# Reordering the first projections of a hybrid attention kernel: the second token pair, the last value weights, and two remainders

## The chip, the cores and the metric

One core of a Trainium2 chip runs the whole program. The metric is the device time of one execution in microseconds (us); the kernel before takes 1420.7 us, the median of three runs between 1420.46 and 1420.71.

The core has five engines with a queue each: TensorE (PE in the profile, its weight loads PEld), VectorE (DVE), ScalarE (ACT), GpSimd (POOL) and SyncE (SP, which issues most of the loads). An engine works through its queue in order; an instruction that needs the result of another engine waits in its place.

## The reference

The layer normalises the input, projects it with one wide matrix, runs two branches on it, merges them by gates, and ends in an MLP and a last normalisation. Only the beginning matters for this change:

```
def hybrid_layer(x, layer, norm1_g, w_in, ...):
    xn = rmsnorm(x, norm1_g[layer])
    u = xn @ w_in[layer].astype(f32)
    c = np.cumsum([SB_WIDTH, SB_WIDTH, SB_WIDTH, HG_WIDTH, HG_WIDTH, HG_WIDTH, HG_WIDTH, D_MODEL])
    q_sb, k_sb, v_sb, f_raw, i_hg, q_hg, g_hg, gate_sb, gate_hg = jnp.split(u, list(c), axis=-1)
    o_sb = stick_breaking_attention(split_heads(q_sb, SB_HEADS), split_heads(k_sb, SB_HEADS),
                                    split_heads(v_sb, SB_HEADS))
    ...
    merged = g_a * (o_sb @ w_o_sb[layer].astype(f32)) + g_b * (o_hg @ w_o_hg[layer].astype(f32))
    h = x.astype(f32) + merged @ w_out[layer].astype(f32)
    ...
    a = jnp.square(jax.nn.relu(hn @ w_ff1[layer].astype(f32)))
    h = h + a @ w_ff2[layer].astype(f32)
    return h
```

There are 1024 tokens of width 1024. `rmsnorm` divides a token by the root of its mean square and multiplies each column by a gain. The first head's queries and keys (64 columns each) and all values (512 columns) are what the first part of the program computes.

## The kernel before

**Two-part numbers.** A float32 operand is split into a high part, rounded to TensorE's `fp32r` format, and a low part, the remainder. A product is three matmuls: high by high, low by high, high by low. The high part is a cast on ScalarE (`hi_copy`, L156), the remainder a subtraction on VectorE (`lo_sub`, L161) that reads the raw tile and the high part.

**The input.** Tokens come in eight blocks of 128 (`x0` to `x7`; block 2 and block 3 are called x_165 and x_169 in the built program). A block's mean square is taken half on ScalarE and half on VectorE (`half_means`), GpSimd raises it to the power -1/2 (`inv_root`, L274), VectorE multiplies the block by that (`norm1`, L664). TensorE transposes it in eight column groups kt of 128 columns (`norm_transpose`, L131), one PSUM bank `xnt` to a group; from there ScalarE writes the high part with the gain applied (`xnh`, L348) and VectorE the low part (`xnl`, L351). A tile of xnh and of xnl holds two groups: 229/230 the groups 0 and 1, 237/238 the groups 2 and 3, 245/246 the groups 4 and 5, 253/254 the groups 6 and 7. Blocks 0 and 1 are the first pair, 2 and 3 the second, 4 to 7 the second half.

**The first job.** `first_job` makes a generator that advances one step at a time. It computes the first head's query/key product `pjqk` (weights `wqk0whi`, `wqk0wlo`) and the values `pjv`, one PSUM bank to a token block. The value weights come in four pieces of two column groups each: raw `wvr`, high `wvh`, remainder `wvl`; piece 0 serves groups 0 and 1, piece 3 the groups 6 and 7. In the kernel before, its steps are: the first pair's query/key (four steps), pieces 0 and 1 of the values of blocks 0 and 1 with the high weights (two steps), the same with the remainders (two steps), the second pair's query/key (four steps), then the values' other pieces and the remaining blocks.

**What sets the order.** The main program calls `st.advance(n, 1)` for n steps between its own parts, and this fixes each queue up to that point. `lo_now` issues subtractions that were put off in `owed_wlo`; before, that is piece 1's `wvl` alone. `turns` chains the instructions of ScalarE and of VectorE in the order in which they are written; `after` records such an order for the compiler and adds no wait on the chip. The loads on SyncE are in the order x0, x1, norm gains, wqk0, wvr 0, x2, wvr 1, x3, wvr 2, wvr 3, x4 to x7.

The main program around the change, before:

```
    st.advance(4, 1)
    u_v.split(2)
    norm1((2, 3), half_means((2, 3)))
    lo_now()
    st.advance(3, 1)
    norm_transpose(xn, 0, 2, 2)
    u_v.split()
    st.advance(5, 1)
```

Of the kernel before, what the change touches and what calls it, by code (L numbers as in the profile page):

```python
# [9 lines left out]
F32 = mybir.dt.float32  # L10
# [4 lines left out]
ALU = mybir.AluOpType  # L15
# [24 lines left out]
def kernel(  # L40
# [19 lines left out]
    nc = tc.nc  # L60
# [14 lines left out]
    def slot(name, dt=F32):  # L75
        return spool.tile([P, 1024], dt, tag="s", name=name)
# [7 lines left out]
    def bank(name):  # L84
        return psum.tile([P, 512], F32, tag="p", name=name)
# [19 lines left out]
    def after(ins, earlier):  # L105
        if earlier is not None and earlier.ins is not ins.ins:
            tc.add_manual_dep(ins.ins, earlier.ins.name, NOSYNC, reason="issue order")
        return ins

    def open_block(name):  # L110
        cur[0] = name
        lane = lanes[name]
        lane.gates = (lane.last,)
        if name == "main":
            lane.ends.append(lane.last)
        else:
            ends = lanes["main"].ends
            lane.gates += tuple(ends[-AHEAD : len(ends) - AHEAD + 1])
# [11 lines left out]
    def transpose(dst, src):  # L130
        return pe(nc.tensor.transpose(dst, src, ident))  # L131
# [7 lines left out]
    last_lo, attended, owed_wlo = [None], [None], []  # L139

    def lo_now(behind=None):
        while owed_wlo:
            after(owed_wlo.pop()(), behind)

    turns = {"on": False, "act": None, "dve": None}

    def in_turn(engine, ins):
        if turns["on"]:
            after(ins, turns[engine])
            turns[engine] = ins  # L150
        return ins
# [3 lines left out]
    def hi_copy(dst, src):  # L155
        hi_last[0] = after(in_turn("act", nc.scalar.copy(dst, src)), hi_behind[0])  # L156

    def lo_sub(dst, src, hi):
        return in_turn(
            "dve",  # L160
            nc.vector.tensor_tensor(out=dst, in0=src, in1=hi.bitcast(F32), op=ALU.subtract),  # L161
        )

    def hi_lo(h, l, src):
        hi_copy(h, src)
        return lo_sub(l, src, h)
# [16 lines left out]
    def halves():  # L183
        return ((i, slice(i * 512, (i + 1) * 512)) for i in range(2))
# [134 lines left out]
            c = (kt % 2) * 512 + (tb % 4) * P  # L319
            return h[:, c : c + P], l[:, c : c + P]  # L320

    def norm_transpose(acts, half, b0, n, between=None):

        banks = {}

        def turn_block(kt, b):
            if kt not in banks:
                banks[kt] = bank(f"xnt{half}{kt}_{b0}")[:, 0 : n * P]
            open_block("main")
            transpose(  # L330
                banks[kt][:, b * P : (b + 1) * P],
                xt[4 * half + b0 + b][:, kt * P : (kt + 1) * P],
            )

        ahead = 6 if between else 0
        for kt in range(ahead):
            turn_block(kt, 0)
        if between:
            between()
        for kt in range(KT):  # L340
            hi, lo = acts.t.get((half, kt // 2)) or acts.make(half, kt // 2)
            cs = slice(kt % 2 * 512 + b0 * P, kt % 2 * 512 + (b0 + n) * P)
            for b in range(n):
                if b > 0 or kt >= ahead:
                    turn_block(kt, b)
            pb = banks[kt]
            g = prm[:, G1 + kt : G1 + kt + 1]
            in_turn("act", nc.scalar.activation(hi[:, cs], pb, AF.Identity, scale=g))  # L348
            in_turn(
                "dve",  # L350
                nc.vector.scalar_tensor_tensor(  # L351
                    out=lo[:, cs],
                    in0=pb,
                    scalar=g,
                    in1=hi[:, cs].bitcast(F32),
                    op0=ALU.mult,
                    op1=ALU.subtract,
                ),
            )

    class Quads:

# [82 lines left out]
    class Unit:  # L445
# [28 lines left out]
        def split(self, upto=None):  # L474
            self.load(upto)
            self.hl = self.hl or []
            for i, r in list(enumerate(self.raw))[len(self.hl) : upto]:
                if self.wide:
                    h = slot(f"{self.name}h{i}", F32R)
                    l = slot(f"{self.name}l{i}", F32R)  # L480
                else:
                    h = wpool.tile([P, 1024], F32R, tag="whi", name=f"{self.name}h{i}")
                    l = wpool.tile([P, 1024], F32R, tag="wlo", name=f"{self.name}l{i}")
                self.hl.append((h, l))
                if self.name == "wf1" or self.name == "wv" and i == 1:
                    hi_copy(h, r)
                    owed_wlo.append(lambda h=h, l=l, r=r: lo_sub(l, r, h))
                    continue
                after(after(hi_lo(h, l, r), last_lo[0]), attended[0])

# [73 lines left out]
    st = Stream()  # L564
# [54 lines left out]
    xn = Acts("xn")  # L619

    def half_means(tbs):
        (l, lc), (r, rc) = halves()
        means = {}
        for tb in tbs:
            t, scr = xt[tb], slot(f"n1scr{tb}")
            ssq = small.tile([P, 1], F32, tag="ssq1", name=f"n1_{tb}_ss", bufs=4)
            in_turn(
                "act",
                nc.scalar.activation(
                    scr[:, lc], t[:, lc], AF.Square, scale=D ** -0.5, accum_out=ssq  # L630
                ),
            )
            ms = mean_square(scr[:, rc], t[:, rc], EPS, f"n1_{tb}")
            in_turn("dve", add(ms, ms, ssq))
            means[tb] = inv_root(ms, f"n1_{tb}")
        return means
# [21 lines left out]
    def norm1(tbs, means=None):  # L658
        for tb in tbs:
            t = xt[tb]  # L660
            r = means[tb] if means else token_rstd(t, f"n1_{tb}", slot(f"n1scr{tb}"))
            in_turn(
                "dve",
                nc.vector.tensor_scalar(out=t, in0=t, scalar1=r, scalar2=None, op0=ALU.mult),  # L664
            )
# [58 lines left out]
    def first_job():  # L724
        name, u_qk, ep = qk_item(0)
        u_qk.__class__ = FirstUnit
        u_v = wide_unit("wv", W_IN, C_V, 512)
        u_v.roomy = range(4)
        open_banks = {}

        def v_part(tb, kt, hi=True, lo=True):
            if kt == 0 and hi:
                open_banks[tb] = bank(f"pjv_{tb}")
            ps = open_banks[tb]
            sh, sl = xn.stat(kt, tb)
            wh, wl = (w[:, kt % 2 * 512 : (kt % 2 + 1) * 512] for w in u_v.hl[kt // 2])
            if hi:
                matmul(ps, sh, wh, start=kt == 0, stop=False)
                matmul(ps, sl, wh, start=False, stop=False)
            if lo:  # L740
                matmul(ps, sh, wl, start=False, stop=kt == KT - 1)

        def v_steps(tb, kts):
            for kt in kts:
                v_part(tb, kt)
                if kt == KT - 1:
                    v_epilogue(open_banks.pop(tb), tb)
                if kt % 2 == 1:
                    yield

        def qk_steps(ps, half, b0, n):
            ts = slice(b0 * P, (b0 + n) * P)
            return proj_half(ps[:, ts], u_qk.hl[0], xn.mov, KT, half, ts=ts)

        def body():
            ps = bank(f"{name}_0")
            yield from qk_steps(ps, 0, 0, 2)
            for hi in (True, False):
                for k0 in (0, 2):
                    for tb in range(2):  # L760
                        for kt in (k0, k0 + 1):
                            v_part(tb, kt, hi, not hi)
                    yield
            yield from qk_steps(ps, 0, 2, 2)
            ep(ps, 0)
            st.prefetch()
            for tb in range(4):
                yield from v_steps(tb, range(4, KT) if tb < 2 else range(KT))
            ps = bank(f"{name}_1")
            yield from qk_steps(ps, 1, 0, 4)  # L770
            ep(ps, 1)
            for tb in range(4, NT):
                yield from v_steps(tb, range(KT))

        return st.add([u_qk], body), u_qk, u_v

    j_first, u_qk0, u_v = first_job()
    j_qk = {0: j_first}

# [1549 lines left out]
    st.advance(4, 1)  # L2329
    u_v.split(2)  # L2330
    norm1((2, 3), half_means((2, 3)))
    lo_now()
    st.advance(3, 1)
    norm_transpose(xn, 0, 2, 2)
    u_v.split()
    st.advance(5, 1)
    norm1(range(4, NT))
    st.advance(8, 1)
    norm_transpose(xn, 1, 0, 4)
# [16 lines left out]
    for i, it in enumerate(items):  # L2356
# [12 lines left out]
        def between():  # L2369
            if before:  # L2370
                values(*before)

        r = turn(*it, between)
# [135 lines left out]
```

## Time and profile before

| | before |
|---|---|
| median of three runs | 1420.7 us |
| the profiled execution | 1420.47 us |
| its span, first to last instruction | 1418.7 us |
| TensorE busy | 1408.6 us, 99% |
| VectorE busy | 1088.1 us, 77% |
| ScalarE busy | 684.6 us, 48% |
| GpSimd busy | 143.3 us, 10% |
| granted TensorE clock | 0.999 of full speed |

The profile is of one execution. Its views list the instructions by engine and group, in the order of time, or by what an engine waited for. In a row of the order of time stand the start, the duration, the engine, the line, the operation, output and inputs by name, shapes and count; in brackets how long the engine had idled before and what ended that. A row with a count above one joins like instructions that follow each other. Matmuls overlap, and their ends are modelled, so the distance between two starts says more than a duration. A row of the waits names the engine and its instruction, what it waited for, the microseconds in total, how often, and the longest. A row of the groups has the busy time and the mean in ns behind the first bar. A row of the stretches has the bounds, the length, the busy time of each engine with its number of instructions, the granted clock, the share of the DMA engines and the GB/s.

### The profile page before, as it was taken

Reading aid. Unit: us, or ns where it says so; the run is one execution under the profiler, and the core shown is the slowest. Engines: PE = TensorE matmul, PEld = TensorE weight load, DVE = VectorE, ACT = ScalarE, POOL = GpSimd, SP = SyncE. Lnnn points to the kernel's source line nnn. Section 1 sums busy time; section 2 is a strip of 40 time slices with the busy share of each in tenths; the row PEclk is TensorE's granted clock in tenths of the full one; section 3 lists DMA queues with packets and bytes.
Section 4 is the critical chain, followed back from the end, with each engine's and each line's share of the span. In section 5 each row is a group of like instructions: output and inputs, shape, how many; then the busy total and the mean of one; then the engine's idle time right before and its main releaser. Section 6 shows DMA issues by size and latency. Waiting matters only on the chain.

```text
span 1418.7 us, 18796 instructions
## 1 busy us (share of the span) xinstructions
PE 1408.6 (99%) x6848; PEld 1184.0 (83%) x6848; DVE 1088.1 (77%) x1494; ACT 684.6 (48%) x1182; POOL 143.3 (10%) x339
## 2 busy tenths in 40 slices
PE   9999999999999999999999999999999999999998
PEld 8888888888888888888888888888888888888886
DVE  7579988988567888887788897677766657768766
ACT  6356676664243554433334764445444443434343
POOL 3012223210011031000000300000000000000031
PEclk9999999999999999999999999999999999999999
DMA  7124445545135685364585514444446974776725
GB/s 238 30 67 127 105 100 98 106 76 155 62 74 167 227 222 182 124 215 156 160 299 193 185 53 170 163 162 139 143 144 239 351 268 152 278 273 240 277 93 187
DMA packets 163173, 237.72 MB, mean 168 GB/s; under 512 B 26332, under 2 KB 93448, under 8 KB 163080
## 3 DMA queue, kind: packets, MB, share of 16 engines
q1 hardware_dynamic: 146056, 190.37, 40.0%
q0 software_dynamic: 11584, 34.61, 10.0%
q10 hardware_dynamic: 5440, 11.54, 2.3%
q8 instruction: 54, 0.88, 0.3%
q14 instruction: 39, 0.32, 0.1%
HBM read 168.32 MB, written 66.06 MB: 165 GB/s over the span
## 4 chain that ended last, share of the span: by engine, by line
PE 98%; DVE 1%; ACT 1%; DMA 0%; issue 0%; POOL 0%; SPq 0%; POOLq 0%; DVEq 0%; ACTq 0%
PE pm L128 21%; PE pX L128 9%; PE pW L128 6%; PE pY L128 6%; PE pjqk L128 6%; PE pga L128 4%; PE gX L128 4%; PE gY L128 4%; PE pjf L128 3%; PE pjq L128 3%; PE pys L128 3%; PE pji L128 3%; PE pyh L128 3%; PE pjv L128 3%; PE po L128 3%; PE z L128 2%
## 5 line engine op out<-in xcount | busy, mean ns | idle before, releaser
L156 ACT CAST whid<-w 128x1024 fp32r<-128x1024 f32 x30 | 31.6, 1054 | 154.4 <-PE pm L128 89.7
L826 DVE TENSOR_TENSOR_SCAN rm<-rm,bits 128x511 f32<-128x511 f32 (+7 forms) x72 | 87.3, 1220 | 17.0 <-ACT rm L804 16.9
L128 PE MATMUL pm<-whid,sh 128*128 128x512 f32 x240 | 93.4, 389 | 0.0
L128 PE MATMUL pm<-wlod,sh 128*128 128x512 f32 x240 | 93.4, 389 | 0.0
L128 PE MATMUL pm<-whid,sl 128*128 128x512 f32 x240 | 93.4, 389 | 0.0
L128 PE MATMUL pm<-tl,sh 128*128 128x512 f32 (+1 forms) x210 | 81.3, 387 | 0.0
L128 PE MATMUL pm<-th,sl 128*128 128x512 f32 (+1 forms) x210 | 81.3, 387 | 0.0
L128 PE MATMUL pm<-th,sh 128*128 128x512 f32 (+1 forms) x210 | 81.3, 387 | 0.0
L161 DVE TENSOR_TENSOR wlod<-w,whid 128x1024 fp32r<-128x1024 f32 x30 | 36.7, 1223 | 54.5 <-ACT whid L156 54.5
L161 DVE TENSOR_TENSOR sl<-sa,sh 128x1024 fp32r<-128x1024 f32 x56 | 68.2, 1218 | 0.3 <-ACT sh L156 0.3
L156 ACT CAST wTh<-pw 128x512 fp32r<-128x512 f32 (+2 forms) x96 | 43.8, 485 | 41.9 <-PE pw L131 41.0
L156 ACT CAST sh<-sa 128x1024 fp32r<-128x1024 f32 x56 | 57.2, 1046 | 7.8 <-DMA sa<-ad 7.8
L2143 POOL TENSOR_SCALAR fss<-fss 128x1 f32<-128x1 f32 x8 | 3.9, 482 | 562.0 <-ACT fsc L2138 561.5
L161 DVE TENSOR_TENSOR wTl<-pw,wTh 128x512 fp32r<-128x512 f32 (+2 forms) x96 | 49.9, 546 | 3.9 <-ACT wTh L156 3.7
L128 PEld LDWEIGHTS pm<-wlod,sh 128*128 128x128 f32 x240 | 45.0, 188 | 9.5
L128 PEld LDWEIGHTS pm<-whid,sl 128*128 128x128 f32 x240 | 45.1, 188 | 9.3
L128 PEld LDWEIGHTS pm<-whid,sh 128*128 128x128 f32 x240 | 45.1, 188 | 9.3
L169 DVE TENSOR_TENSOR bt<-bt,rm 128x511 f32<-128x511 f32 (+7 forms) x72 | 48.9, 685 | 3.5
L804 ACT ACTIVATE rm<-z 128x511 f32<-128x511 f32 (+4 forms) x96 | 48.0, 500 | 5.5 <-PE z L128 2.9
L128 PE MATMUL pX<-sqh,t1l 128*128 128x512 f32 x128 | 49.9, 390 | 0.0
L128 PE MATMUL pX<-sql,t1h 128*128 128x512 f32 x128 | 49.9, 390 | 0.0
L128 PE MATMUL pX<-sqh,t1h 128*128 128x512 f32 x128 | 49.8, 389 | 0.0
(930 smaller groups left out, 4432.4 us busy)
## 6 DMA issues: line engine op xcount, KB each, us to landing
w<-in_w_ff_dram SPq DMA_DIRECT2D x72, 512.0 KB, 4.7
sa<-ad SPq DMA_DIRECT2D x52, 512.0 KB, 6.4
ad<-a SPq DMA_DIRECT2D x32, 256.0 KB, 4.5
ad<-s SPq DMA_DIRECT2D x16, 512.0 KB, 3.3
tw<-in_w_out_dram POOLq DMA_DIRECT2D x24, 256.0 KB, 4.5
pr<-pd SPq DMA_DIRECT2D x10, 512.0 KB, 6.0
x<-in_x_dram SPq DMA_DIRECT2D x8, 512.0 KB, 7.8
xnl<-xnh POOLq DMA_DIRECT2D x8, 512.0 KB, 6.4
```

Of the source, the lines that this page charges most:

```text
L128: return pe(nc.tensor.matmul(*a, **k))
L156: hi_last[0] = after(in_turn("act", nc.scalar.copy(dst, src)), hi_behind[0])
L161: nc.vector.tensor_tensor(out=dst, in0=src, in1=hi.bitcast(F32), op=ALU.subtract),
L169: return nc.vector.tensor_tensor(out=out, in0=a, in1=b, op=ALU.mult)
L804: nc.scalar.activation(rm[:, s0 + c0 - 1 : s0 + m - 1], z[:, c0:m], AF.Sigmoid, scale=-0.125)
L826: sc = nc.vector.tensor_tensor_scan(out=rr, data0=rr, data1=bits[:, 1024 - nk + a : 1024 - nk + b][:, ::-1], initial=rm[:, b : b + 1] if i ...
L2143: nc.gpsimd.tensor_scalar(out=ssq, in0=ssq, scalar1=1.0 / D, scalar2=EPS, op0=ALU.mult, op1=ALU.add)
```

## The change

Five edits, all in the first some 25 us of the program. Inside `first_job` the last quarter of the values with remainders (piece 1, both blocks) moves behind the second pair's query/key. `norm_transpose` gets a call after each column group, and the main program advances the first job there, after groups 4, 6 and 7. The raw value pieces 2 and 3 are cast before these transposes and not behind them. Piece 2's remainder goes to GpSimd, written behind block 3's scaling; pieces 1 and 3 have theirs put off, and `lo_now`, which now takes the oldest first, stands behind the transposes.

```diff
     def lo_now(behind=None):
         while owed_wlo:
-            after(owed_wlo.pop()(), behind)
+            after(owed_wlo.pop(0)(), behind)
...
-    def norm_transpose(acts, half, b0, n, between=None):
+    def norm_transpose(acts, half, b0, n, between=None, then=None):
...
                     op1=ALU.subtract,
                 ),
             )
+            if then:
+                then(kt)
...
-                if self.name == "wf1" or self.name == "wv" and i == 1:
+                if self.name == "wf1" or self.name == "wv" and i in (1, 3):
                     hi_copy(h, r)
                     owed_wlo.append(lambda h=h, l=l, r=r: lo_sub(l, r, h))
                     continue
+                if self.name == "wv" and i == 2:
+                    hi_copy(h, r)
+                    ins = nc.gpsimd.tensor_tensor(
+                        out=l, in0=r, in1=h.bitcast(F32), op=ALU.subtract
+                    )
+                    after(ins, turns["dve"])
+                    continue
                 after(after(hi_lo(h, l, r), last_lo[0]), attended[0])
...
+        def v_quarter(hi, k0):
+            for tb in range(2):
+                for kt in (k0, k0 + 1):
+                    v_part(tb, kt, hi, not hi)
+
...
         def body():
             ps = bank(f"{name}_0")
             yield from qk_steps(ps, 0, 0, 2)
-            for hi in (True, False):
-                for k0 in (0, 2):
-                    for tb in range(2):
-                        for kt in (k0, k0 + 1):
-                            v_part(tb, kt, hi, not hi)
-                    yield
+            for hi, k0 in ((True, 0), (True, 2), (False, 0)):
+                v_quarter(hi, k0)
+                yield
             yield from qk_steps(ps, 0, 2, 2)
+            v_quarter(False, 2)
+            yield
             ep(ps, 0)
             st.prefetch()
...
     u_v.split(2)
     norm1((2, 3), half_means((2, 3)))
+    u_v.split()
+    st.advance(3, 1)
+    norm_transpose(xn, 0, 2, 2, then=lambda kt: st.advance(1, 1) if kt in (4, 6, 7) else None)
     lo_now()
-    st.advance(3, 1)
-    norm_transpose(xn, 0, 2, 2)
-    u_v.split()
-    st.advance(5, 1)
+    st.advance(2, 1)
     norm1(range(4, NT))
```

On TensorE, before, around the last transposes of the second pair (each `xnt` number is one column group; pjv_316 and pjv_321 are the values of blocks 0 and 1, wvl_295 is piece 1's remainder):

```order
L131 MATMUL xnt_2_363<-ident,x_165 128x128
L131 MATMUL xnt_2_363<-ident,x_169 128x128
L131 MATMUL xnt_2_368<-ident,x_165 128x128
L131 MATMUL xnt_2_368<-ident,x_169 128x128
L128 MATMUL pjv_316<-wvl_295,xnh_237 128x512
L131 MATMUL xnt_2_373<-ident,x_165 128x128
L131 MATMUL xnt_2_373<-ident,x_169 128x128
L128 MATMUL pjv_316<-wvl_295,xnh_237 128x512
L128 MATMUL pjv_321<-wvl_295,xnh_237 128x512 x2
L128 MATMUL pjqk_0_265<-xnh_229,wqk0whi 128x256
```

The same place in the changed program, from the transposes of group 4 (xnt_2_364) to those of group 6 (xnt_2_380):

```order
L131 MATMUL xnt_2_364<-ident,x_165 128x128
L131 MATMUL xnt_2_364<-ident,x_169 128x128
L128 MATMUL pjqk_0_265<-xnh_229,wqk0whi 128x256
L128 MATMUL pjqk_0_265<-xnl_230,wqk0whi 128x256
L128 MATMUL pjqk_0_265<-xnh_229,wqk0wlo 128x256
L128 MATMUL pjqk_0_265<-xnh_229,wqk0whi 128x256
L131 MATMUL xnt_2_375<-ident,x_165 128x128
L128 MATMUL pjqk_0_265<-xnl_230,wqk0whi 128x256
L128 MATMUL pjqk_0_265<-xnh_229,wqk0wlo 128x256
L131 MATMUL xnt_2_375<-ident,x_169 128x128
L131 MATMUL xnt_2_380<-ident,x_165 128x128
L131 MATMUL xnt_2_380<-ident,x_169 128x128
```

The second pair's query/key products of groups 0 and 1 now stand among the transposes. Behind these rows come the six products of groups 2 and 3, the two transposes of group 7, the twelve products of groups 4 to 7, and then the four value products with wvl_295, which before stood among the transposes.

On VectorE, before, from the scaling of the second pair to its first low parts:

```order
L664 TENSOR_SCALAR x_165<-x_165,n_2_y 128x1024
L664 TENSOR_SCALAR x_169<-x_169,n_3_y 128x1024
L161 TENSOR_TENSOR wvl_295<-wvr_167,wvh_294 128x1024
L351 SCALAR_TENSOR_TENSOR xnl_230<-xnt_2_338,prm,xnh_229 128x256
L351 SCALAR_TENSOR_TENSOR xnl_230<-xnt_2_343,prm,xnh_229 128x256
```

And in the changed program, from the pair's last low parts (groups 5 to 7) to the scaling of block 4:

```order
L351 SCALAR_TENSOR_TENSOR xnl_246<-xnt_2_375,prm,xnh_245 128x256
L351 SCALAR_TENSOR_TENSOR xnl_254<-xnt_2_380,prm,xnh_253 128x256
L351 SCALAR_TENSOR_TENSOR xnl_254<-xnt_2_391,prm,xnh_253 128x256
L161 TENSOR_TENSOR wvl_295<-wvr_167,wvh_294 128x1024
L161 TENSOR_TENSOR wvl_320<-wvr_173,wvh_319 128x1024
L673 TENSOR_SCALAR x_175<-x_175,n_4_y 128x1024
```

Piece 1's remainder moved from before the eight low parts to behind them; of the two remainders that stood there (pieces 2 and 3) only piece 3's, wvl_320, is left.

On GpSimd, in the changed program, from the powers of the second pair to those of block 4:

```order
L274 TENSOR_TENSOR n_2_y<-n_2_ms,expo 128x1
L274 TENSOR_TENSOR n_3_y<-n_3_ms,expo 128x1
L493 TENSOR_TENSOR wvl_316<-wvr_171,wvh_315 128x1024
L265 TENSOR_SCALAR n_4_ss<-n_4_ss 128x1
L269 TENSOR_TENSOR n_4_y<-n_4_ss,expo 128x1
```

The third row is new: piece 2's remainder, which waits on the chip for its raw load and its cast and for nothing on VectorE. On ScalarE the casts wvh_315 and wvh_319 of pieces 2 and 3 now stand before the pair's eight high parts and not behind them. The loads on SyncE keep their order. Behind this stretch every engine's queue has the same instructions in the same order as before.

## The prediction

> **What bounds the kernel now.** I read the page first, then the list of what TensorE waited for, then the order of time around the only place where that list names a wait inside the changed stretch.
>
> ```profile
> span 1418.7 us, 18796 instructions
> PE 1408.6 (99%) x6848; PEld 1184.0 (83%) x6848; DVE 1088.1 (77%) x1494; ACT 684.6 (48%) x1182; POOL 143.3 (10%) x339
> PE 98%; DVE 1%; ACT 1%; DMA 0%; issue 0%; POOL 0%; SPq 0%; POOLq 0%; DVEq 0%; ACTq 0%
> PE warm L128 <- POOL ident masks.py:199: 2.2, 1, 2.2
> PE po L128 <- DVE wTl L161: 0.3, 1, 0.3
> PE pjqk L128 <- DVE xnl L351: 0.3, 1, 0.3
> PE xnt L131 <- DVE xnl L351: 0.2, 1, 0.2
> ```
>
> TensorE is busy for 99% of the span and 98% of the chain of waits lies on it. Its four listed waits are all there are in 1418.7 us, and one of them (0.2 us, the transposes waiting for VectorE's xnl) lies where the change works. The change issues the same 6848 matmuls, so it can only add or remove TensorE idling, and behind about 25 us no wait is left that could swallow a delay or give a gain. So I ask when the matmul at 23.97 below (the first product of value piece 2) can start in the changed order.
>
> TensorE in the order of time:
>
> ```profile
> 17.82 1.25 PE L131 MATMUL xnt<-ident,x 128*128 128x128 f32 x10
> 19.28 0.83 PE L131 MATMUL xnt<-ident,x 128*128 128x128 f32 x4 [0.21 <-DVE xnl L351]
> 19.86 0.48 PE L128 MATMUL pjv<-wvl,xnh 128*128 128x512 f32 x1
> 20.18 0.38 PE L131 MATMUL xnt<-ident,x 128*128 128x128 f32 x2
> 20.32 0.94 PE L128 MATMUL pjv<-wvl,xnh 128*128 128x512 f32 x3
> 21.09 0.28 PE L128 MATMUL pjqk<-xnh,wqk0whi 128*128 128x256 f32 x1
> ...
> 23.85 0.28 PE L128 MATMUL pjqk<-xnh,wqk0wlo 128*128 128x256 f32 x1
> 23.97 0.40 PE L128 MATMUL pjv<-wvh,xnh 128*128 128x512 f32 x1
> ...
> 34.20 0.39 PE L128 MATMUL pjv<-wvh,xnh 128*128 128x512 f32 x1
> 34.42 0.39 PE L128 MATMUL pjv<-wvh,xnl 128*128 128x512 f32 x1
> 34.88 3.65 PE L131 MATMUL xnt<-ident,x 128*128 128x128 f32 x32
> 38.29 0.48 PE L128 MATMUL pjv<-wvh,xnh 128*128 128x512 f32 x1
> ```
>
> Matmuls overlap, so their price is the distance of starts, not the printed duration. Transposes: 38.29 - 34.88 = 3.41 us for 32, 0.107 each. Query/key products: 23 steps from 21.09 to 23.85, so 2.76 / 23 = 0.12. Value products: 34.42 - 34.20, about 0.227 with its neighbours. The stretch holds 16 transposes, 4 value products with wvl and 24 query/key products: 1.71 + 0.91 + 2.88 = 5.50 us of work, in 23.97 - 17.82 = 6.15 us. The idling is 0.65 us. That is all that interleaving can win.
>
> **What feeds TensorE there.** Each transposed column group kt goes through ScalarE (xnh, L348) and then VectorE (xnl, L351).
>
> ```profile
> 14.86 0.24 ACT L629 ACTIVATION_READ_ACCUMULATOR n1scr<-x 128x1 f32 x1
> 18.23 0.47 ACT L348 ACTIVATE xnh<-xnt,prm 128x256 fp32r<-128x256 f32 x1 [3.13 <-PE xnt L131]
> 18.23 3.03 ACT L348 ACTIVATE xnh<-xnt,prm 128x256 fp32r<-128x256 f32 x8 [3.13 <-PE xnt L131]
> 21.10 2.05 ACT L156 CAST wvh<-wvr 128x1024 fp32r<-128x1024 f32 x2
> 16.93 0.75 DVE L664 TENSOR_SCALAR x<-x,n_y 128x1024 f32<-128x1024 f32 x1
> 17.60 1.22 DVE L161 TENSOR_TENSOR wvl<-wvr,wvh 128x1024 fp32r<-128x1024 f32 x1
> 18.74 3.23 DVE L351 SCALAR_TENSOR_TENSOR xnl<-xnt,prm,xnh 128x256 fp32r<-128x256 f32 x8
> 21.49 0.47 DVE L351 SCALAR_TENSOR_TENSOR xnl<-xnt,prm,xnh 128x256 fp32r<-128x256 f32 x1
> 22.23 2.36 DVE L161 TENSOR_TENSOR wvl<-wvr,wvh 128x1024 fp32r<-128x1024 f32 x2 [0.27 <-ACT wvh L156]
> ```
>
> ScalarE's pace is (3.03 - 0.47) / 7 = 0.365 us a group, VectorE's (21.49 - 18.74) / 7 = 0.393, and a single one takes 0.47. Eight xnl need 3.23 us whatever TensorE does. The first xnl at 18.74 starts as soon as the first xnh ends (18.23 + 0.47 = 18.70); the wvl subtraction in front of it, which ends at 18.82, did not hold it.
>
> **The change, part by part.** (1) *Piece 1's wvl moves on VectorE from before the eight xnl to behind them.* In front it cost the xnl nothing, so they start at 18.74 as now. Behind them it is late: without any other delay VectorE reaches it at 21.49 + 0.39 = 21.88 and ends at 21.88 + 1.22 = 23.10. Its four value products now stand behind the query/key products.
>
> (2) *Query/key products among the transposes.* TensorE runs ten transposes from 17.82 to 18.90, the first query/key product at 18.91, and waits with the second for the first xnl, to 19.27 (before, transposes waiting on that xnl restarted at 19.28). Then, at the steps above: kt 1's first product at 19.51, transposes of kt 5 at 19.63 and 19.98 with two products between, kt 6 at 20.09 and 20.20, six products of kt 2 and 3 from 20.31, transposes of kt 7 at 21.03 and 21.14, kt 4 and 5 from 21.25 to 21.97. A pair is ready about 0.29 us behind its last transpose (second transpose at 17.93, xnh at 18.23). So kt 7 reaches ScalarE at 21.44, where ScalarE's pace alone would have taken it at about 20.8. Its xnh ends at 21.93, its xnl runs from 21.95 to 22.43. TensorE needs that at 22.45 and does not wait noticeably; its last query/key product starts at 22.61 and ends its step at 22.73. But VectorE is now late by 21.95 - 21.49 = 0.46 us.
>
> (3) *The new wait.* wvl of piece 1 starts at 21.95 + 0.39 = 22.34 and is there at 23.58; TensorE, ready at 22.73, idles until 23.62 (0.04 to see it). Four products, 0.91: the matmul now at 23.97 starts at 24.53. The sum is 24.53 - 23.97 = **+0.56 us**. Queued behind the waiting product is everything on TensorE.
>
> (4) *ScalarE's two casts move from 21.10 to 15.10*, into its idle 3.13 us: 2.05 us from 15.10 to 17.15 if the raw pieces are there.
>
> ```profile
> 7.26 0.95 SPq L136 DMA_DIRECT2D wvr<-in_w_in_dram  x2
> 8.26 3.00 SPq L136 DMA_DIRECT2D x<-in_x_dram  x4
> 2.00:15.40 13.40, 12.77 (x75) 11.61 (x76) 9.85 (x25) 9.43 (x22) 2.34 (x7) 1.00 1.04 352
> ```
>
> Up to piece 3 the queue holds nine half-megabyte loads (four x, four wvr, one wqk0), 4.72 MB; the last row moved 13.4 x 352 = 4.72 MB by 15.40. With up to 1 us until a load is seen, the last cast ends at 16.4 + 1.1 = 17.5, before 18.23. Cost nothing; had the load come only at 18, xnh would be late by some 0.9. ScalarE's squares of blocks 4 to 7, which stood behind the casts, move ahead; TensorE transposes those blocks only at 34.88 and does not see it.
>
> (5) *Piece 2's wvl on GpSimd.* No row has GpSimd subtracting 128x1024. The tie to block 3's scaling joins two engines and orders the program text only; no wait on it is in the instruction (it waits for the raw load and for ScalarE).
>
> ```profile
> 24.29 0.36 POOL L265 TENSOR_SCALAR n_ss<-n_ss 128x1 f32<-128x1 f32 x1 [7.39 <-ACT n1scr L295]
> 24.73 0.55 POOL L269 TENSOR_TENSOR n_y<-n_ss,expo 128x1 f32<-128x1 f32 x1
> 25.37 0.75 POOL L265 TENSOR_SCALAR n_ss<-n_ss 128x1 f32<-128x1 f32 x1
> 25.32 0.75 DVE L664 TENSOR_SCALAR x<-x,n_y 128x1024 f32<-128x1024 f32 x1 [0.72 <-POOL n_y L269]
> 15.13 1.76 POOL L274 TENSOR_TENSOR n_y<-n_ms,expo 128x1 f32<-128x1 f32 x2 [7.39 <-DVE n_ms L1284]
> L813 POOL MEMSET bits<- 128x1024 uint8 x1 | 1.0, 952 | 0.0
> masks.py:199 POOL TENSOR_SCALAR_AFFINE_SELECT ident<-ident 128x128 f32<-128x128 f32 x1 | 0.3, 287 | 0.0
> ```
>
> Below, 0.95 us (1024 columns written only); above, 8 x 0.287 = 2.3 us for eight times the columns of the one row that reads and writes f32 tiles. I take 2.3, since that row is nearest in kind; nothing excludes 3. (By the Trainium skill, "GPSIMD Engine Reference", section 3.1, 2048 columns of a two-input fp32 operation take 4497 ns; my estimate from it is 2.25, the same sum.) The product that needs it is the third behind 24.53, at 24.98: from a start at 17.7 even 7 us are covered.
>
> When does it start? GpSimd's 0.36 us operation took 0.75 when it began 0.05 us after VectorE's scaling and ended 0.05 behind it (26.12 against 26.07): GpSimd is held while VectorE scales. After GpSimd's n_y ends at 25.28, VectorE's scaling starts at 25.32, GpSimd's own next at 25.37. The same pair meets at 16.89: scaling of block 3 at 16.93, the subtraction at 16.98. VectorE is first and GpSimd runs from 17.7 to 20.0, under xnl.
>
> The Trainium skill ("SBUF — State Buffer", section "SBUF: two separate sides") says that the port pair of the two goes to whoever starts first, for the whole instruction. The held 0.75 us row agrees for VectorE first; the other order no row shows. By that page ("Who interferes with whom") a VectorE operation with one SBUF input, as xnl has beside its PSUM one, is not held; no row here has both.
>
> **The rivals.** *A, no loss:* ScalarE gets kt 7 earlier (the transposes overtake, or the query/key steps are shorter) and xnl keeps its pace. Then wvl ends at 23.10, TensorE continues at 23.14, the matmul starts at 24.05: +0.08, 1420.8 us. For it: the margin is a few tenths; against: kt 7's transposes stand behind twelve products and four transposes at known steps. Anything faster needs wvl by 22.7, which eight xnl from 18.74 forbid. *B, GpSimd first:* it begins before block 3's scaling and holds it. Scaling from 16.98 + 2.3 = 19.28 to 20.03, the transposes of block 3 at 20.07, not 17.93: 2.14 late, all told 2.7 us, 1423.4; with 3 us, 1424.1. It decides once GpSimd starts 0.05 us earlier than I read. Against it: VectorE won such a meeting in the rows above. *C, GpSimd holds xnl:* the first xnl waits from 18.74 to 20.0, 1.3 us; the pace then covers kt 7's lateness (0.46), so wvl ends at 20.0 + 8 x 0.393 + 1.22 = 24.4 and the matmul starts at 25.3: +1.4, 1422.1. For it, the held row above; against it, that row's VectorE work is all in SBUF, xnl's is half in PSUM. *D, a gain over 0.2%:* would need a second place that moves; the wait list has none.
>
> **How the numbers follow.** The sum stands against the profiled execution's 1420.47 us (span 1418.7): 1421.03. The median of the runs is 0.23 above that, so 1421.3. Chances: forecast 0.60, A 0.18, C 0.12, B 0.08, D 0.02. The forecast with A spans 1420.5 to 1421.7; with C and the unknown GpSimd price the upper end goes to 1422.7, the lower to 1420.3 for steps read 0.2 us too long. 0.2% is 2.8 us, about what a measurement of this kernel can tell from no change. Slower than that is only B with a long GpSimd operation and what I have not seen, 0.07; faster 0.02; within, 0.91.
>
> **What would show it.** Right: a wait of some 0.9 us of TensorE's pjv for VectorE's wvl near 22.7 to 23.6, kt 7's xnh alone behind a gap on ScalarE, GpSimd's subtraction starting at about 17.7, and later matmuls all shifted by 0.5 to 0.6. A: no gap before the last xnh. B: block 3's scaling starts behind GpSimd's subtraction. C: xnl stretched or starting at 20. Wrong altogether: a wait in the list that lies beyond 26 us, or the casts ending after 18.23.

## The result, and the profile after

The changed kernel takes 1423.37 us (median of 22 runs, 1422.69 to 1424.86) against 1420.82 us before (22 runs, 1420.33 to 1421.09): 2.55 us longer, a ratio of 1.0018 with a 95% interval of 1.0013 to 1.0024. The forecast was 1421.3 us, the range ended at 1422.7, so the prediction was wrong. Rival B, GpSimd first, had been priced at 1423.4 us and given 0.08.

The page of the changed kernel and its list of what TensorE waited for (engine and line, then what it waited for, the microseconds in total, how often, the longest):

```profile
span 1421.6 us, 18796 instructions
PE 1409.5 (99%) x6848; PEld 1184.4 (83%) x6848; DVE 1088.8 (77%) x1493; ACT 684.8 (48%) x1182; POOL 143.9 (10%) x340
PE warm L128 <- POOL ident masks.py:199: 2.2, 1, 2.2
PE xnt L131 <- DVE x L673: 1.8, 1, 1.8
PE pjv L128 <- DVE wvl L161: 0.6, 1, 0.6
PE po L128 <- DVE wTl L161: 0.3, 1, 0.3
```

Two waits are new. The one of 0.6 us for piece 1's remainder was forecast. The one of 1.8 us was not: the transposes wait for the scaling of an input block. The first and the last row of the waits are those of before, so the loss lies in the front. The changed kernel in the order of time, TensorE first, then VectorE, GpSimd and ScalarE:

```profile
17.82 0.27 PE L131 MATMUL xnt<-ident,x 128*128 128x128 f32 x1
19.87 1.20 PE L131 MATMUL xnt<-ident,x 128*128 128x128 f32 x9 [1.78 <-DVE x L673]
20.83 0.36 PE L128 MATMUL pjqk<-xnh,wqk0whi 128*128 128x256 f32 x1
...
25.73 1.21 PE L128 MATMUL pjv<-wvl,xnh 128*128 128x512 f32 x4 [0.63 <-DVE wvl L161]
26.78 0.40 PE L128 MATMUL pjv<-wvh,xnh 128*128 128x512 f32 x1
...
16.29 3.53 DVE L673 TENSOR_SCALAR x<-x,n_y 128x1024 f32<-128x1024 f32 x2 [0.17 <-POOL n_y L274]
17.11 2.70 DVE L673 TENSOR_SCALAR x<-x,n_y 128x1024 f32<-128x1024 f32 x1
20.74 3.04 DVE L351 SCALAR_TENSOR_TENSOR xnl<-xnt,prm,xnh 128x256 fp32r<-128x256 f32 x7 [0.93 <-ACT xnh L348]
24.06 0.48 DVE L351 SCALAR_TENSOR_TENSOR xnl<-xnt,prm,xnh 128x256 fp32r<-128x256 f32 x1 [0.27 <-ACT xnh L348]
24.46 2.35 DVE L161 TENSOR_TENSOR wvl<-wvr,wvh 128x1024 fp32r<-128x1024 f32 x2
...
15.31 1.76 POOL L274 TENSOR_TENSOR n_y<-n_ms,expo 128x1 f32<-128x1 f32 x2 [7.70 <-DVE n_ms L1297]
16.74 2.52 POOL L493 TENSOR_TENSOR wvl<-wvr,wvh 128x1024 fp32r<-128x1024 f32 x1
...
15.13 2.20 ACT L156 CAST wvh<-wvr 128x1024 fp32r<-128x1024 f32 x2
23.55 0.47 ACT L348 ACTIVATE xnh<-xnt,prm 128x256 fp32r<-128x256 f32 x1 [0.31 <-PE xnt L131]
```

The scaling of block 3 begins at 17.11 and takes 2.70 us where it took 0.75. GpSimd's subtraction is listed from 16.74 to 19.26, and the scaling ends at 19.81, 0.55 us behind it. The first transpose of the pair (block 2) starts at 17.82 as before, the second, of block 3, at 19.87. From the pair's first transpose to the first product of piece 2 it is now 26.78 - 17.82 = 8.96 us, where it was 6.15. I measure every run below by this distance, since the start of the stretch moves by a few tenths of a us from one execution to the next.

The Trainium skill ("SBUF — State Buffer", section "SBUF: two separate sides") says that whichever of the two starts first has the shared port pair for the whole instruction, and the other blocks. This trace shows the half of it that the trace of before could not: 0.75 us became 2.70 us for VectorE.

### The profile page after: what moved, and what is told of

It is laid out like the page before. It is cut to its first block, busy times and chain, and to the rows that moved or that the text cites. A ratio compares the mean times of both kernels' runs of the same rounds, so it can differ in the third digit from the quotient of the medians.

```text
span 1421.6 us, 18796 instructions
## 1 busy us (share of the span) xinstructions
PE 1409.5 (99%) x6848; PEld 1184.4 (83%) x6848; DVE 1088.8 (77%) x1493; ACT 684.8 (48%) x1182; POOL 143.9 (10%) x340
## 4 chain that ended last, share of the span: by engine, by line
PE 98%; DVE 1%; ACT 1%; issue 0%; POOL 0%; POOLq 0%; DVEq 0%; ACTq 0%
PE pm L128 21%; PE pX L128 9%; PE pW L128 6%; PE pY L128 6%; PE pjqk L128 6%; PE pga L128 4%; PE gX L128 4%; PE gY L128 4%; PE pjf L128 3%; PE pjq L128 3%; PE pys L128 3%; PE pji L128 3%; PE pyh L128 3%; PE pjv L128 3%; PE po L128 3%; PE z L128 2%
```

## The experiments

Three theories were on record before the first four runs: that GpSimd's subtraction holds the scaling because it starts first (1), that GpSimd slows whatever VectorE does beside it (2), and that the new order costs it and not GpSimd (3). All times are medians of 11 runs (one repeat is a single run), against 1420.8 us for the kernel before in the same jobs; a ratio is to that kernel, with its 95% interval.

**A true wait.** GpSimd's remainder waits on the chip for the scaling of block 3 (`SYNC` is a dependency that becomes a semaphore wait, where `after` records the order alone).

```diff
-                    after(ins, turns["dve"])
+                    tc.add_manual_dep(ins.ins, turns["dve"].ins.name, SYNC, reason="port")
```

> The changed kernel, but GpSimd's remainder really waits on the chip for VectorE's scaling of block 3. Theory 1 (the shared port goes to whoever starts first, and GpSimd's subtraction started before the scaling): the subtraction starts at about 17.75 us, the scaling takes 0.75 us again instead of 2.70, the last transposes of the pair begin at 17.9, and what is left is the late remainder of piece 1: the first product of piece 2 starts at 24.5 us (26.78 in the changed kernel, 23.97 before), time 1421.1 to 1421.6 us. Theory 2 (GpSimd slows whatever VectorE does beside it): the low parts xnl are stretched or start only at 20.2 us, the product starts at 25.3 us or later, time 1422.0 us or more. Theory 3 (the new order costs it, not GpSimd): no change, 1423.4 us.

It took 1421.39 us. The order of time (VectorE, GpSimd, TensorE):

```profile
15.75 1.58 DVE L674 TENSOR_SCALAR x<-x,n_y 128x1024 f32<-128x1024 f32 x2 [0.17 <-POOL n_y L275]
18.41 3.04 DVE L352 SCALAR_TENSOR_TENSOR xnl<-xnt,prm,xnh 128x256 fp32r<-128x256 f32 x7 [1.09 <-ACT xnh L349]
...
17.46 2.38 POOL L494 TENSOR_TENSOR wvl<-wvr,wvh 128x1024 fp32r<-128x1024 f32 x1 [0.92 <-ACT wvh L157]
...
17.49 1.25 PE L132 MATMUL xnt<-ident,x 128*128 128x128 f32 x10
23.40 1.19 PE L129 MATMUL pjv<-wvl,xnh 128*128 128x512 f32 x4 [0.63 <-DVE wvl L162]
24.43 0.40 PE L129 MATMUL pjv<-wvh,xnh 128*128 128x512 f32 x1
```

Both scalings end after 1.58 us, the subtraction starts 0.13 us behind them, and ten transposes run through. (The row names ScalarE's cast as what released GpSimd, but that had ended at 16.10; GpSimd's queue waited on VectorE's semaphore until 17.37, 0.04 us behind the scaling.) The distance is 24.43 - 17.49 = 6.94 us: 2.02 of the 2.81 us are gone, with one wait and nothing else changed. That is theory 1; theory 3 can explain at most the 0.79 us that stay. The subtraction runs from 17.46 to 19.84, beside the first low parts; seven of these take 3.04 us, as in the changed kernel, where they run after it. So theory 2 and rival C are out as well.

**All remainders on VectorE.**

```diff
-                if self.name == "wf1" or self.name == "wv" and i in (1, 3):
+                if self.name == "wf1" or self.name == "wv" and i in (1, 2, 3):
                     hi_copy(h, r)
                     owed_wlo.append(lambda h=h, l=l, r=r: lo_sub(l, r, h))
                     continue
-                if self.name == "wv" and i == 2:
...
```

> The changed kernel with piece 2's remainder on VectorE, put off with pieces 1 and 3 behind the low parts; nothing on GpSimd. Theory 1: the first product of piece 2 starts at 24.5 us as in the run with the true wait, TensorE waits 0.9 us for piece 1's remainder, time 1421.1 to 1421.6 us. Theory 2: the same. Theory 3 (the new order costs it): 1423.4 us.

1421.49 us. The order of time (VectorE, one row; TensorE):

```profile
22.54 3.49 DVE L161 TENSOR_TENSOR wvl<-wvr,wvh 128x1024 fp32r<-128x1024 f32 x3
...
17.86 1.29 PE L131 MATMUL xnt<-ident,x 128*128 128x128 f32 x10
...
22.68 0.38 PE L128 MATMUL pjqk<-xnl,wqk0whi 128*128 128x256 f32 x1
22.90 0.28 PE L128 MATMUL pjqk<-xnh,wqk0wlo 128*128 128x256 f32 x1
23.81 1.20 PE L128 MATMUL pjv<-wvl,xnh 128*128 128x512 f32 x4 [0.63 <-DVE wvl L161]
24.84 0.39 PE L128 MATMUL pjv<-wvh,xnh 128*128 128x512 f32 x1
```

A distance of 6.98 us, and the same wait of 0.63: with GpSimd properly tied or not used at all, the same 0.8 us is left over the kernel before. The times agree (1421.39 and 1421.49); the intervals of their ratios to before (0.9995 to 1.0013 and 0.9996 to 1.0013) include 1, so it is the distance that shows this rest. By the sum of the prediction it was to be 24.53 - 17.82 = 6.71 us, so both runs are 0.2 to 0.3 us longer than forecast; the run with the true wait met its 24.5 only because its stretch began 0.33 us earlier. The wait was expected at 0.9 us and is listed with 0.63; the list counts from the modelled end of the product before it (22.90 + 0.28 = 23.18).

**GpSimd's part alone.** The kernel before, with pieces 2 and 3 cast ahead, piece 2's remainder on GpSimd, and piece 3's put off; TensorE's order and piece 1's remainder as before.

```diff
     lo_now()
+    u_v.split()
     st.advance(3, 1)
     norm_transpose(xn, 0, 2, 2)
-    u_v.split()
+    lo_now()
     st.advance(5, 1)
```

> The kernel before with one part of the change: pieces 2 and 3 cast ahead, piece 2's remainder on GpSimd with its tie in the program text, piece 3's put off behind the low parts; TensorE's order as before, piece 1's remainder in front of the low parts. Theory 1: block 3's scaling is held until about 19.8 us, the transposes come 2.1 us late, and the first product of piece 2 starts at 25.9 to 26.2 us (23.97 before), time 1422.7 to 1423.1 us. Theory 3 (the new order of TensorE and of piece 1's remainder costs it): as before, 1420.8 us.

1423.80 us, between 1422.62 and 1424.98, at two levels: five runs from 1422.6 to 1423.1, six from 1423.8 to 1425.0. The order of time of the profiled execution, at 1422.62 (VectorE, GpSimd, TensorE):

```profile
15.93 3.53 DVE L671 TENSOR_SCALAR x<-x,n_y 128x1024 f32<-128x1024 f32 x2 [0.17 <-POOL n_y L274]
16.38 2.53 POOL L491 TENSOR_TENSOR wvl<-wvr,wvh 128x1024 fp32r<-128x1024 f32 x1
17.65 0.27 PE L131 MATMUL xnt<-ident,x 128*128 128x128 f32 x1
19.52 1.20 PE L131 MATMUL xnt<-ident,x 128*128 128x128 f32 x9 [1.60 <-DVE x L671]
25.72 0.40 PE L128 MATMUL pjv<-wvh,xnh 128*128 128x512 f32 x1
```

The two scalings take 3.53 us again, and the distance is 8.07: 1.92 us more than before, as theory 1 has it, by a little less than the 2.1 expected. The lower level is that; of the upper one, 1.5 us above by the medians of the two groups, I had no profile, and ran the same kernel once more:

> The kernel with GpSimd's remainder alone once more, for its profile: its times lay at two levels, 1422.6 to 1423.0 and 1423.8 to 1425.0 us. If this profile lies on the upper level, the extra 1.2 to 1.5 us should be found in it: in the first 30 us as a longer hold of the scaling, or as matmuls at a lower clock behind TensorE's idling; if on the lower level, the second level stays open.

It came out at 1422.63 us, on the lower level again, with the same distance (8.07). What the upper level is stays open. The recorded mean clock of TensorE is 0.998 or 0.999 of full speed in the five runs and 0.997 or 0.998 in the six, and a thousandth of 1423 us is 1.4 us, so a slightly lower clock may be all of it; that is not shown. One of the 22 runs of the changed kernel (1424.86) lies as far above the others.

**Half the subtraction.**

```diff
+                    cs = slice(0, 512)
                     ins = nc.gpsimd.tensor_tensor(
-                        out=l, in0=r, in1=h.bitcast(F32), op=ALU.subtract
+                        out=l[:, cs], in0=r[:, cs], in1=h[:, cs].bitcast(F32), op=ALU.subtract
                     )
                     after(ins, turns["dve"])
+                    cr = slice(512, 1024)
+                    owed_wlo.append(
+                        lambda h=h, l=l, r=r: lo_sub(l[:, cr], r[:, cr], h[:, cr])
+                    )
```

> The changed kernel with GpSimd subtracting only the first 512 of piece 2's 1024 columns; VectorE subtracts the others behind piece 1's. Theory 1: GpSimd's subtraction takes 1.2 to 1.4 us instead of 2.52, still starts at about 16.74, so block 3's scaling ends at about 18.6 us instead of 19.82, and 1.2 us of the loss comes back: time 1422.0 to 1422.4 us. If the hold does not go with the length of the subtraction: 1423.4 us. Theory 3: 1423.4 us.

1422.31 us (1.0011, 1.0002 to 1.0020). The order of time (VectorE, GpSimd, TensorE):

```profile
16.06 2.45 DVE L678 TENSOR_SCALAR x<-x,n_y 128x1024 f32<-128x1024 f32 x2 [0.17 <-POOL n_y L274]
16.52 1.45 POOL L494 TENSOR_TENSOR wvl<-wvr,wvh 128x512 fp32r<-128x512 f32 x1
17.79 0.27 PE L131 MATMUL xnt<-ident,x 128*128 128x128 f32 x1
25.48 0.40 PE L128 MATMUL pjv<-wvh,xnh 128*128 128x512 f32 x1
```

The subtraction ends at 17.97 and the scaling at 18.51, 0.54 behind it, the same lag as with the full length (0.55). The subtraction's 1.45 us are just over the 1.2 to 1.4 expected. The distance is 7.69 us, 1.27 less than with 1024 columns. The hold goes with the length of GpSimd's instruction.

**Piece 1's remainder in front again**, on top of the run with all remainders on VectorE.

```diff
+    lo_now()
     u_v.split()
     st.advance(3, 1)
     norm_transpose(xn, 0, 2, 2, then=lambda kt: st.advance(1, 1) if kt in (4, 6, 7) else None)
     lo_now()
```

> The run with all remainders on VectorE, with one edit more: piece 1's remainder stands in front of the low parts again, where it ended at 18.8 us in the kernel before. Theory 1 (what is left of the loss, some 0.65 us, is TensorE's wait for that remainder, late behind the low parts): the wait of pjv for wvl goes, the first product of piece 2 starts some 6.0 us behind the first transpose of the pair (6.15 before, 6.98 in the run on VectorE), time 1420.5 to 1420.8 us. Rival 4 (the late transposes of group 7, and with them the low parts, cost it): the wait stays in another place, the distance stays at 6.6 us or more, time 1421.2 us or more.

1420.52 us (ratio to before 0.9998, 0.9989 to 1.0007). The order of time (VectorE, TensorE):

```profile
18.59 3.04 DVE L351 SCALAR_TENSOR_TENSOR xnl<-xnt,prm,xnh 128x256 fp32r<-128x256 f32 x7
...
17.66 1.25 PE L131 MATMUL xnt<-ident,x 128*128 128x128 f32 x10
22.79 1.09 PE L128 MATMUL pjv<-wvl,xnh 128*128 128x512 f32 x4
23.71 0.39 PE L128 MATMUL pjv<-wvh,xnh 128*128 128x512 f32 x1
```

The wait is gone and the distance is 6.05 us, 0.93 less for one subtraction put back. So the second loss was the late remainder; the late transposes of group 7, still there, cost no more than the interleaving gains.

**The gap filled.** On top of that, the four products with piece 1's remainder go back ahead of the query/key steps, so that they stand behind the transposes of group 4.

```diff
-            for hi, k0 in ((True, 0), (True, 2), (False, 0)):
+            for hi, k0 in ((True, 0), (True, 2), (False, 0), (False, 2)):
                 v_quarter(hi, k0)
                 yield
             yield from qk_steps(ps, 0, 2, 2)
-            v_quarter(False, 2)
-            yield
```

> As the run with piece 1's remainder in front, and the four products with that remainder moved ahead of the query/key steps: they fill the place behind the transposes of group 4, where TensorE waits for the first low part; one query/key step each stands behind the transposes of groups 6 and 7. Theory 1: no wait is left in the stretch, it takes the 5.5 us that its work adds up to (6.15 before), time 1420.1 to 1420.4 us, faster than both kernels by the few tenths that the idling before allows. Rival 4: group 7's transposes come later still, the low parts end late, distance 6.0 us or more, time 1420.7 us or more.

1420.11 us (1419.74 to 1420.38; ratio 0.9996, 0.9987 to 1.0005), below both kernels. The order of time (VectorE, one row; TensorE):

```profile
17.64 1.22 DVE L161 TENSOR_TENSOR wvl<-wvr,wvh 128x1024 fp32r<-128x1024 f32 x1
...
17.69 1.29 PE L131 MATMUL xnt<-ident,x 128*128 128x128 f32 x10
18.91 1.21 PE L128 MATMUL pjv<-wvl,xnh 128*128 128x512 f32 x4
...
23.47 0.40 PE L128 MATMUL pjv<-wvh,xnh 128*128 128x512 f32 x1
```

5.78 us, not the 5.5 expected, but 0.37 below before. The list has no wait of TensorE left in the stretch, but the first product with the remainder starts at 18.91, 0.05 us behind the end of VectorE's subtraction (17.64 + 1.22 = 18.86), where ten transposes at 0.107 would have let it start at 18.76; the four products take 1.05 us (to 19.96), as they do behind a wait, and not the 0.91 of the sum. These two make up the difference. The median lies 0.68 us below that of before in the same job, and all 11 runs lie at or below 1420.38 while those of before begin at 1420.31; the interval of the ratio still includes 1, so the gain is likely rather than proved.

**The same with GpSimd, truly tied.** This run was to let VectorE's subtraction for piece 1, with two inputs in SBUF, meet GpSimd's.

```diff
     lo_now()
     u_v.split()
...
+                    tc.add_manual_dep(ins.ins, turns["dve"].ins.name, SYNC, reason="port")
```

> As the run that fills the gap, with piece 2's remainder on GpSimd and a true wait on VectorE's scaling of block 3; VectorE subtracts piece 1's remainder (two inputs in SBUF) at that same time. Theory 1 (whoever starts first holds a two-input subtraction too): VectorE is first, GpSimd's subtraction starts or ends some 1.2 us later than in the run with the true wait (17.46 to 19.84 there, beside low parts only), nothing is lost: time as the run that fills the gap. If GpSimd comes first: piece 1's remainder takes some 2.4 us longer, low parts start at 20.2 us, time 1422 us. If two-input subtractions do not hold each other: both run at their own length side by side.

1420.15 us (0.9996, 0.9987 to 1.0005). The order of time (VectorE, GpSimd, TensorE):

```profile
16.06 1.58 DVE L674 TENSOR_SCALAR x<-x,n_y 128x1024 f32<-128x1024 f32 x2 [0.17 <-POOL n_y L275]
17.55 1.22 DVE L162 TENSOR_TENSOR wvl<-wvr,wvh 128x1024 fp32r<-128x1024 f32 x1
18.73 3.00 DVE L352 SCALAR_TENSOR_TENSOR xnl<-xnt,prm,xnh 128x256 fp32r<-128x256 f32 x7
...
18.91 2.40 POOL L494 TENSOR_TENSOR wvl<-wvr,wvh 128x1024 fp32r<-128x1024 f32 x1 [2.06 <-ACT xnh L349]
...
17.80 1.25 PE L132 MATMUL xnt<-ident,x 128*128 128x128 f32 x10
23.38 0.40 PE L129 MATMUL pjv<-wvh,xnh 128*128 128x512 f32 x1
```

The two did not meet. `turns["dve"]` holds the VectorE instruction written last, and with `lo_now()` in front of `u_v.split()` that is piece 1's subtraction and not block 3's scaling, so the true wait is on the subtraction. The trace agrees: GpSimd's queue waits on VectorE's semaphore until 18.81, 0.04 us behind the end of the subtraction (17.55 + 1.22 = 18.77), the same 0.04 as behind the scaling in the run with the true wait. (The row names ScalarE as the releaser, but ScalarE had cast piece 2 long before.) GpSimd's late start, which theory 1 of the expectation forecast, is this wait, and the run says nothing on whether two such subtractions hold each other. GpSimd takes its 2.40 us beside the low parts, whose pace does not change, and the distance is 23.38 - 17.80 = 5.58 us. Nothing is lost by GpSimd here, and nothing is gained: what it takes off VectorE was not on the path.

## Why the prediction was wrong

**What bounds it: right.** No wait beyond 26 us came or went, and what the front lost appears in the time: 2.81 us of distance, 2.55 us of median.

**(1) Piece 1's remainder: right.** In front it cost the low parts nothing (in the run with it in front they start at 18.59, 0.93 us behind the first transpose; in the two runs without it there 0.92 and 0.96), behind them it is late, and putting it back took 0.93 us.

**(2) and (3) The interleaving and the new wait: the mechanism right, the size 0.25 us short.** The gap of ScalarE before the last xnh (0.31 us), of VectorE before the last xnl (0.27) and TensorE's wait for the remainder are there as described. The sum was +0.56 us; the true wait and the run on VectorE measure 6.94 - 6.15 = +0.79 and 6.98 - 6.15 = +0.83. In the latter VectorE's subtraction starts 22.54 - 17.86 = 4.68 us behind the first transpose, where I had 22.34 - 17.82 = 4.52, and the four products behind the wait take 24.84 - 23.81 = 1.03 us instead of 0.91. I had priced a matmul behind a wait like any other; here restarts were about 0.1 us dearer, once behind the first xnl (19.36 to 19.59 in that run, 0.23 us for a step of 0.12) and once here. A slip of 0.02 works the other way: 22.34 + 1.22 is 23.56, where the sum has 23.58.

**(4) The casts: right.** They ended at 17.33, and ScalarE was idle again until the first xnh.

**(5) GpSimd: this step failed.** It read: "VectorE is first and GpSimd runs from 17.7 to 20.0, under xnl." The second half held once the wait was made true (17.46 to 19.84, xnl undisturbed). The first did not. I had taken the order of the two from rows in which GpSimd's next operation began 0.09 us behind its last. In the changed kernel the subtraction is listed from 16.74, while the small power for block 3 had not ended (15.31 + 1.76 = 17.07). VectorE's scaling of block 2 ends at about 17.04 (16.29 and its usual 0.75), that of block 3 starts at 17.11, since it needs this power; GpSimd's subtraction was ahead of it. When it took hold is in no row. The end of block 2's scaling, or of this power, fits better than the listed start: from the end of that scaling to the end of the subtraction it is 2.22 us here, 2.23 in GpSimd's part alone and 2.23 in its repeat, while the listed lengths are 2.52, 2.53 and 2.45. In all four profiles in which GpSimd had no true wait, it came first. 2.02 us of the loss hang on that, shown by the true wait that removes them, by GpSimd's part alone that adds 1.92 to the kernel before, and by the half length that gives 1.27 back. Why GpSimd's instruction is listed from before the end of the one in front of it here, and was not in the rows that I quoted, no run shows.

Of the rivals, B is what happened, by its mechanism and nearly by its price (2.14 + 0.56 = 2.70 against 2.02 + 0.79 = 2.81). Its sign looks different in the rows: block 3's scaling does not start behind the subtraction, its row is stretched over it. B was underrated: the sentence of the Trainium skill, the missing wait on the chip and a margin of 0.05 us were all in the prediction, and rows of another pair of instructions outweighed them. A did not occur in the changed order, and C is excluded.

## What to carry to other kernels

An order written into the program text between two engines is no wait on the chip; where two engines exclude each other for the length of an instruction, the one that must go first needs a true wait in front of the other, or the other's instruction has to be short. A margin of 0.05 us from one kind of instruction doesn't carry over to another, so a rival that hangs on it deserves a large chance. And a piece of work moved out of a place where it cost nothing needs its new deadline checked: here the subtraction that moved from in front of the low parts to behind them ate what the interleaving could win.

## What was not expected of the hardware

GpSimd's subtraction of 128x1024 took 2.38 and 2.40 us when undisturbed, against 1.22 us on VectorE. It held VectorE's scaling (2.70 us instead of 0.75, ending 0.55 us behind it) and did not touch VectorE's operations with one input in PSUM and one in SBUF (seven in 3.04 us with and without it). The third case, a VectorE operation with two SBUF inputs, stands in the changed kernel's trace, with a small operation of GpSimd, the power for block 4:

```profile
25.81 1.41 POOL L269 TENSOR_TENSOR n_y<-n_ss,expo 128x1 f32<-128x1 f32 x1
```

It began while VectorE's two remainder subtractions ran (24.46 + 2.35 = 26.81), ended 0.41 us behind them and took 1.41 us; in the kernel before and in GpSimd's part alone, with no such subtraction beside it, the same operation took 0.55. So VectorE, when first, holds GpSimd there too, and its subtractions kept their usual length. GpSimd first against such a subtraction occurs in no run. The Trainium skill ("SBUF — State Buffer", section "Who interferes with whom") tells these three cases apart in the same way. The two levels of the kernel with GpSimd's part alone, about 1.5 us apart, remain unexplained.
